# Local attention of a hybrid decoder: when the sixth query tile's weights are split, and how ten weight tiles get their low parts

## The chip, the cores and the metric

The kernel runs on one core of a Trainium2 chip. The metric is the device time of one execution in microseconds. Five engines work on queues of their own and meet only at semaphores: TensorE (PE, with its weight loads as PEld), VectorE (DVE), ScalarE (ACT), GpSimd (POOL) and SyncE (SP). SP issues nearly all transfers; POOL issues those that add what they carry onto what lies at their destination.

## The reference, cut to what matters

The model is a two-layer decoder over 528 tokens (16 of them meta tokens) of width 1024. Each layer is a feed-forward block, a token mixer and another feed-forward block. The mixer of the second layer is sliding-window attention over 128 tokens, with keys and values made earlier, and the change lies in its query and output projections:

```python
def swa_mixer(hn, w_q, sinks, w_out, k, v, cos, sin):
    q = (hn @ w_q).reshape(B, L, N_KV_HEADS, GROUP, HEAD_DIM)
    q = (apply_partial_rope(q, cos, sin) * (HEAD_DIM ** -0.5)).transpose(0, 2, 3, 1, 4)
...
    s = jnp.einsum('bkgnqd,bknsd->bkgnqs', q_blk, k_band)
...
    p = sink_softmax(s, mask, sink_b[None, :, :, None, None, None])
    o_real = jnp.einsum('bkgnqs,bknsd->bkgnqd', p.astype(v.dtype), v_band).reshape(B, N_KV_HEADS, GROUP, S, HEAD_DIM)
    o = jnp.concatenate([o_meta, o_real], axis=3).transpose(0, 3, 1, 2, 4).reshape(B, L, N_Q_HEADS * HEAD_DIM)
    return o @ w_out
```

Everything is float32. The kernel gets that precision from TensorE by splitting each operand into a high part, which TensorE takes in its fast float32 form (fp32r), and a low part, the rest: a product is then high by high, low by high and high by low, three matrix products.

## The kernel before, in words

**Weights.** All weights are cut into units in the order of their use (`units`). Here a unit is a tile of 128 by 1024 numbers: one query tile (`w_q`, eight of them, two heads each) or one tile of the output weights (`swa_out`, eight). A unit comes from memory by SP into two raw tiles of 512 columns (`load_unit`, L293; there are 11 raw tiles). Each half is then split by `split_part` (L235): ACT copies the raw half into the high part of a new tile (L237), DVE subtracts that from the raw half into the low part (L238). These tiles `w` come from a pool of 32 slots, which also holds queries, scores and other work.

**The planner.** The program is written out in full when the kernel is built. `Flow` (L64) is a clock that matrix products advance by an assumed cost (`mm`, L164: 512 columns of fp32r cost 512/2400 us), and a heap of jobs that fall due at times of that clock. What is due is written into the program between the products (`flow.pump`, after every three products of a unit). The engines' queues therefore hold the work in about the order of the due times; a scheduler may move an instruction that isn't ready behind later ones.

`split_unit` (L241) is the job of one unit: 2.2 us after the assumed end of its transfer it falls due, it may have to wait for the operand `x.built[1]`, for a gap of 2.2 us to the half before it (`gap[0]`, which is GAP from L1337 on), and for room (`slot`, L225). Room is a count of half-tiles: `set_ahead(n)` (L220) lets the planner ask for n halves beyond those that were given back by `done_w` (L347), and hold n at a time. `next_w` (L325) takes the next unit for TensorE; the planner's clock goes on, and other due jobs are written out, until that unit's job is done.

**The stage.** `swa` (L1213) calls `set_ahead(10)`, then `x_first` (L500) for the first four query tiles: their weights are there, `set_ahead(2 * first_ahead)` with first_ahead=5 leaves room for one tile more, the fifth, whose split waits for `x.built[1]`. The first four tiles are multiplied for two groups of 256 tokens, which follow each other as the normalized input is built; then `done_w(4)` gives eight halves of room, and `x_units` (L477) multiplies tiles five to eight for all 512 tokens, eight times three products of 512 columns each. Tiles that are done go through `rope` (L1150): DVE shuffles and multiplies by cosines (L1153, L1154), POOL multiplies by sines and adds (L1155, L1156). POOL's rope of the second token group needs the cosines and sines `csq`, which DVE has first to scale with the norm of that group (L1231).

`soft` (L1244) is one query tile's scores and softmax: four blocks of score products `sc` (one step of two products each), their reduction on DVE (L1267), exponentials on ACT (L1274), and the multiplication by the inverse sum (L1290), one head on DVE and the other on POOL. `core` (L1292) transposes the result on TensorE (`pt`, `pp`, L177), copies it (L1309, L1310) and multiplies by the values (`o`). The first scores fall due 2.0 us after the ropes of the first four tiles, so scores, query products and later transposes and output products stand mixed in TensorE's queue. `out_proj` (L551) multiplies by the output weights, in two halves of four units each.

**Transfers that add.** The feed-forward blocks already use them: `split_pair` (L254) builds sums of two weight blocks with `onto`, a transfer issued by POOL with `accum_op=ALU.add` (L270).

Of the kernel before, what the change touches and what calls it, by code (L numbers as in the profile page):

```python
# [9 lines left out]
F32 = mybir.dt.float32  # L10
F32R = mybir.dt.float32r
I32 = mybir.dt.int32
AF = mybir.ActivationFunctionType
ALU = mybir.AluOpType
# [4 lines left out]
KD = 8  # L19
# [108 lines left out]
def trunk_kernel(ctx: ExitStack, tc, a, out):  # L128
    nc = tc.nc
    pe, act, dve, pool, sp = nc.tensor, nc.scalar, nc.vector, nc.gpsimd, nc.sync  # L130
    flow = Flow()
# [15 lines left out]
    def ps(name):  # L147
        return pp.tile([P, 512], F32, tag="ps", name=name)

    def pair_tile(name, dt=F32R):  # L150
        return hp.tile([P, 2, TOK], dt, tag="pair", name=name)
# [8 lines left out]
    def gain(layer, i, k):  # L160
        c = V_GAIN + layer * 48 + i * 8 + k
        return vec[:, c : c + 1]
# [19 lines left out]
    gap, turn = [0.0], [0.0]  # L182
# [6 lines left out]
    units = []  # L189
    for layer in range(2):  # L190
        for f in range(2):
            for lo, hi in FF_CHUNKS:
                for t in range(lo, hi):
                    pair = [a["w_in"][layer, f, t, 0], a["w_in"][layer, f, t, 1]]
                    units += pair if lo == 0 else [pair]
                if lo < LAST:
                    units += [a["w_out"][layer, f, m, :, lo * P : hi * P] for m in range(KD)]
                else:
                    units += [a["w_last"][layer, f, i] for i in range(NLAST)]
            if f == 0 and layer == 0:  # L200
                units += [a["gla_in"][u] for u in GLA_ORDER]
                units += [a["gla_out"][m] for m in range(KD)]
            elif f == 0:
                units += [a["w_q"][u] for u in range(KD)]
                units += [a["swa_out"][i] for i in range(KD)]
            elif layer == 0:
                units += [a["w_kv"][u] for u in range(4)]

    costs = [7 if isinstance(u, list) else -(-u.shape[-1] // 512) for u in units]
    loaded = []  # L210
# [9 lines left out]
    def set_ahead(n, slots=None):  # L220
        ahead[0], limit[0] = n, slots or n
        room[0].finish(flow)
        room[0] = Job(None)

    def slot(i):  # L225

        while live[0] + sum(n for j, n in owed.items() if j < i) >= limit[0]:
            yield room[0]
        live[0] += 1
        owed[i] -= 1  # L230

    def raw_tile(name):
        return rp.tile([P, 512], F32, tag="raw", name=name)

    def split_part(i, raw, m):  # L235
        w = pair_tile(f"w{i}_{len(loaded[i])}")
        act.activation(w[:, 0, :m], raw[:, :m], AF.Copy)  # L237
        hold(dve.tensor_tensor(w[:, 1, :m], raw[:, :m], w[:, 0, :m].bitcast(F32), op=ALU.subtract))  # L238
        loaded[i].append(w)

    def split_unit(i, raws, x):  # L241
        yield 2.2
        if x is not None:
            yield x.built[1]
        for raw, m in raws:
            if gap[0]:
                turn[0] = max(turn[0] + gap[0], flow.clock)
                yield turn[0] - flow.clock
            yield from slot(i)
            bound[0] = x and x.low  # L250
            split_part(i, raw, m)
            bound[0] = None
# [66 lines left out]
    def prefetch():  # L319
        while len(loaded) < cap[0] and asked[0] + costs[len(loaded)] <= freed[0] + ahead[0]:  # L320
            if isinstance(units[len(loaded)], list) and chains[0] == CHAINS:
                break
            load_unit()

    def next_w():  # L325
        used[0] += 1
        prefetch()
        flow.until(lambda: len(loaded) >= used[0])
        flow.wait(split_jobs[used[0] - 1])
        return loaded[used[0] - 1]  # L330
# [16 lines left out]
    def done_w(n=1):  # L347
        free_slots(sum(costs[released[0] : released[0] + n]))
        released[0] += n
# [150 lines left out]
    def x_first(x, nu, evac, opening=False, behind=(), first_ahead=8):  # L500
        behind = list(behind)
        ws = [] if opening else [next_w() for _ in range(nu)]
        set_ahead(8 if opening else 2 * first_ahead)
        jobs = []

        def drain(gi, g, some, pst):
            yield x.rjob[gi]
            if not opening:
                yield x.built[1]
            for i, p in zip(some, pst):  # L510
                bound[0] = None if opening else x.low
                evac(i, g, p)
                bound[0] = None
                yield 0.6

        both = range(nu)
        order = [(0, both[: nu // 2]), (0, both[nu // 2 :])] if opening else [(0, both)]
        for gi, some in order + [(1, both)]:
            g = x.groups[gi]
            n = g[1]  # L520
            while len(ws) <= some[-1]:
                ws.append(next_w())
            shared = n <= 256
            if shared:
                banks = [ps(f"x{used[0]}_{i}_{gi}") for i in some[::2]]
                pst = [banks[i // 2][:, i % 2 * 256 : i % 2 * 256 + n] for i in range(len(some))]
            else:
                pst = [ps(f"x{used[0]}_{i}_{gi}")[:, :n] for i in some]
            for k in range(KD):
                if k == 1 and not opening and gi == 1:  # L530
                    cap[0] = len(units)
                    behind_x[0] = x
                    prefetch()
                x.need(gi, k)
                mm3s([(p, ws[i]) for i, p in zip(some, pst)], k, x.tiles[k], g, k == 0, k == KD - 1, shared)
            behind_x[0] = None
            flow.until(lambda: x.rjob[gi] is not None)
            jobs.append(flow.spawn(drain(gi, g, some, pst)))
            if opening and gi == 0 and some[-1] == nu - 1:
                cap[0] = len(units)  # L540
                prefetch()
            if behind:
                flow.spawn(behind.pop(0))
        done_w(nu)
        return jobs
# [666 lines left out]

    def swa(x, kv, finish):  # L1213
        kz, vt, vmz = kv
        set_ahead(10)
        with tc.tile_pool(name="ap", bufs=1) as ap:
            away = ap.tile([P, WIN], F32, name="away")
            sp.dma_start(away, a["away"])
# [112 lines left out]
                softs.append(flow.spawn(soft(u, [*after, *softs[max(u - 2, 0) : max(u - 1, 0)]])))  # L1331
                cores.append(flow.spawn(core(u)))

            drained = x_first(x, 4, evac, first_ahead=5)
            for u in range(4):
                attend(u, *drained)
            gap[0] = GAP  # L1337
# [15 lines left out]
    x = Operand("l0f0", lambda k: gain(0, 0, k), L0)  # L1353
# [19 lines left out]
    raws = [[raw_tile(f"raw{i}_{c}") for c in (0, 512)] for i in range(2)]  # L1373
# [33 lines left out]
    x = nxt  # L1407
    nxt, fin = into("l0f1", 0, 3, False, lambda k: gain(0, 4, k), L0)
    gla(x, fin)
    x = nxt  # L1410
# [4 lines left out]
    with tc.tile_pool(name="kp", bufs=1) as kp:  # L1415
        x = Operand("l1f0", lambda k: gain(1, 0, k), L1)
# [11 lines left out]
        x = nxt  # L1428
# [96 lines left out]
```

## Time and profile before

| | us |
|---|---|
| median of three runs (1869.71 to 1871.39) | 1869.87 |
| the profiled execution, its own time | 1868.85 |
| its span, first instruction to last | 1867.0 |
| TensorE busy in the span | 1848.1 |
| DVE busy in the span | 1349.2 |
| ACT busy in the span | 1002.0 |
| POOL busy in the span | 315.2 |

The profile is of one execution. Times in its views are microseconds from the start of the span. L165 is the line of the helper that makes every matrix product, so products are told apart by their tiles: `x<-x_l1m,w` are the query products of this stage (those of 512 columns belong to tiles five to eight), `sc` the scores, `pt` and `pp` the transposes, `y<-so,w` the output projection. In the same way `w<-raw` at L237 and L238 are the two instructions of a split. The stage's query products begin at 1350.69 and its last output products end near 1506.

### The profile page before, as it was taken

To read this page: it belongs to the slowest core of one execution; us is meant where nothing else is said; L and a number is where in the kernel's file an instruction comes from. 1 tells how busy PE (TensorE), PEld (TensorE's weight loads), DVE (VectorE), ACT (ScalarE), POOL (GpSimd) and SP (SyncE) were. 2 spreads that over 40 slices of the span, in tenths; PEclk is the share of its full clock that TensorE was granted. 3 is DMA by queue.
4 is the path that set the end of the run, shared out by engine and by line. 5 is a ranking of instruction groups with operands and counts; after the bars stand their busy time and mean duration, and the time that the engine had idled before them with its cause. 6 is when DMAs were issued, how large, how long until landed. Compare 5 with 4: busy or idle time off the path is not lost.

```text
span 1867.0 us, 36799 instructions
## 1 busy us (share of the span) xinstructions
PE 1848.1 (99%) x14158; PEld 1762.7 (94%) x14158; DVE 1349.2 (72%) x2679; ACT 1002.0 (54%) x2179; POOL 315.2 (17%) x370
## 2 busy tenths in 40 slices
PE   8999999999999999999999999999999999999998
PEld 8999999999999999999999898989977898989897
DVE  7884757786574988484789685758799589858484
ACT  6662636564465666262665563636556566626363
POOL 2101010320001310101033011010353231010101
PEclk9999999999999999999999999999999999999999
DMA  5655655312113255555652356565411215565561
GB/s 198 146 152 143 153 147 159 125 58 80 46 58 114 69 136 154 137 150 149 163 165 58 102 150 161 145 161 158 131 56 48 80 37 134 161 150 155 145 175 46
DMA packets 132528, 231.31 MB, mean 124 GB/s; under 512 B 14848, under 2 KB 26624, under 8 KB 132352
## 3 DMA queue, kind: packets, MB, share of 16 engines
q1 hardware_dynamic: 111328, 191.07, 32.2%
q0 software_dynamic: 20736, 37.76, 12.9%
q8 instruction: 111, 1.82, 0.4%
q14 instruction: 65, 0.53, 0.1%
q10 hardware_dynamic: 288, 0.13, 0.0%
HBM read 226.80 MB, written 2.10 MB: 123 GB/s over the span
## 4 chain that ended last, share of the span: by engine, by line
PE 89%; DVE 6%; ACT 3%; issue 1%; DMA 0%; POOL 0%; SPq 0%; DVEq 0%; ACTq 0%; POOLq 0%
PE y L165 29%; PE a L165 21%; PE x L165 17%; PE c L165 10%; PE d L165 5%; PE o L165 1%; PE e L165 1%; PE yt L165 1%; PE po L165 1%; DVE w L238 1%; ACT w L237 1%; PE sc L165 1%; DVE H L457 1%; PE ps L165 0%; PE pt L177 0%
## 5 line engine op out<-in xcount | busy, mean ns | idle before, releaser
L270 POOL DMA_DIRECT2D raw<-in_w_in x144 | 125.8, 940 | 973.8 <-DMA raw<-in_w_in 366.1
L165 PE MATMUL y<-hidl0f,w 128*128 128x256 f32 (+1 forms) x2112 | 260.4, 285 | 0.0
L165 PEld LDWEIGHTS y<-hidl0f,w 128*128 128x128 f32 x2112 | 258.6, 188 | 0.2
L238 DVE TENSOR_TENSOR w<-raw,w 128x512 fp32r<-128x512 f32 x376 | 241.3, 669 | 23.6 <-ACT w L237 21.4
L265 DVE TENSOR_TENSOR w_s<-raw,w_s 128x512 fp32r<-128x512 f32 x288 | 195.3, 689 | 80.5 <-ACT w_s L264 78.3
L264 ACT ACTIVATE w_s<-raw 128x512 fp32r<-128x512 f32 x288 | 177.6, 625 | 110.4 <-DVE raw L280 69.9
L165 PE MATMUL y<-hidl1f,w 128*128 128x512 f32 (+1 forms) x1200 | 233.1, 354 | 0.0
L165 PEld LDWEIGHTS y<-hidl1f,w 128*128 128x128 f32 x1200 | 195.1, 188 | 32.8 <-DVE w L238 0.3
L237 ACT ACTIVATE w<-raw 128x512 fp32r<-128x512 f32 x376 | 206.6, 586 | 33.6 <-PE y L165 27.9
L265 DVE TENSOR_TENSOR w<-raw,w 128x512 fp32r<-128x512 f32 x216 | 145.6, 688 | 37.1 <-ACT w L264 35.1
L264 ACT ACTIVATE w<-raw 128x512 fp32r<-128x512 f32 x216 | 130.5, 621 | 46.5 <-PE y L165 45.4
L165 PE MATMUL x<-x_l0m,w 128*128 128x272 f32 (+1 forms) x1152 | 151.9, 289 | 0.0
L165 PEld LDWEIGHTS x<-x_l0m,w 128*128 128x128 f32 x1152 | 143.4, 188 | 1.6 <-ACT R_l0m L375 0.4
L585 DVE TENSOR_TENSOR Y<-y,Y 128x256 f32<-128x256 f32 (+2 forms) x160 | 75.6, 479 | 83.8 <-PE y L165 83.6
L165 PE MATMUL a<-zl0f_t,w_s 128*128 128x264 f32 x864 | 117.2, 285 | 0.0
L165 PE MATMUL a<-zl1f_t,w_s 128*128 128x256 f32 x864 | 114.6, 282 | 0.6 <-ACT c L878 0.4
L165 PEld LDWEIGHTS a<-zl0f_t,w_s 128*128 128x128 f32 x864 | 110.1, 188 | 0.0
L165 PEld LDWEIGHTS a<-zl1f_t,w_s 128*128 128x128 f32 x864 | 107.2, 188 | 1.7 <-ACT c L878 1.6
L394 POOL TENSOR_TENSOR acc_post<-acc_post,sq_post 128x256 f32<-128x256 f32 (+1 forms) x72 | 61.2, 850 | 275.8 <-ACT sq_post L393 272.9
L165 PE MATMUL x<-x_l0f,w 128*128 128x256 f32 (+1 forms) x768 | 98.3, 290 | 6.8 <-ACT w L237 5.9
L165 PEld LDWEIGHTS x<-x_l0f,w 128*128 128x128 f32 x768 | 96.4, 192 | 7.7 <-ACT w L237 5.9
L165 PE MATMUL x<-x_l1f,w 128*128 128x256 f32 (+1 forms) x576 | 92.1, 320 | 0.0
(386 smaller groups left out, 3364.5 us busy)
## 6 DMA issues: line engine op xcount, KB each, us to landing
raw<-in_w_in SPq DMA_DIRECT2D x424, 256.0 KB, 3.7
raw<-in_w_in POOLq DMA_DIRECT2D x144, 256.0 KB, 4.8
raw<-in_w_out SPq DMA_DIRECT2D x96, 256.0 KB, 3.5
raw<-in_w_last SPq DMA_DIRECT2D x48, 256.0 KB, 3.4
raw<-in_gla_in SPq DMA_DIRECT2D x48, 256.0 KB, 3.1
raw<-in_w_out SPq DMA_DIRECT2D x64, 128.0 KB, 2.9
raw<-in_gla_out SPq DMA_DIRECT2D x16, 256.0 KB, 2.8
raw<-in_w_q SPq DMA_DIRECT2D x16, 256.0 KB, 3.9
```

The lines of the kernel that those rows point to most:

```text
L165: inst = pe.matmul(o, lhs, rhs, start=start, stop=stop, skip_group_check=onto)
L237: act.activation(w[:, 0, :m], raw[:, :m], AF.Copy)
L238: hold(dve.tensor_tensor(w[:, 1, :m], raw[:, :m], w[:, 0, :m].bitcast(F32), op=ALU.subtract))
L264: act.activation(w[:, 0, :512], src, AF.Copy)
L265: dve.tensor_tensor(w[:, 1, :512], src, w[:, 0, :512].bitcast(F32), op=ALU.subtract)
L270: pool.dma_start(dst, src, accum_op=ALU.add)
L394: pool.tensor_tensor(sums[0][:, :n], sums[0][:, :n], t[:, :n], op=ALU.add)
L457: dve.tensor_tensor(h, t, h, op=ALU.add)
L585: dve.tensor_tensor(y, p[:, :n], y, op=ALU.add)
```

## The change

The room in the attention stage grows from ten halves to twelve: `set_ahead(12)`, and first_ahead=6, so that the sixth query tile is asked for together with the fifth. Ten units (`lifted`: the last two query tiles, and the eight tiles of output weights) are no longer split by `split_part`. The new `lift` writes for each half the high part by ACT, as before, then by a second ACT copy of scale -1 the negated high part where the low part will lie, and has POOL issue a transfer that adds the weights from memory onto it: minus high plus weight is the low part. The halves of lifted units follow each other at 1.5 us of the planner's clock in place of the gap of 2.2 us, and a lifted unit counts as done 5.0 us after its last issue. The raw halves are still fetched by SP, since the high part is copied from them.

```diff
@@ -202,6 +202,7 @@
             elif f == 0:
                 units += [a["w_q"][u] for u in range(KD)]
+                lifted = range(len(units) - KD + 6, len(units) + KD)
                 units += [a["swa_out"][i] for i in range(KD)]
@@ -238,10 +239,25 @@
+    def lift(i, raws):
+        for c, (raw, m) in enumerate(raws):
+            turn[0] = max(turn[0] + 1.5, flow.clock)
+            yield turn[0] - flow.clock
+            yield from slot(i)
+            w = pair_tile(f"w{i}_{c}")
+            act.activation(w[:, 0, :m], raw[:, :m], AF.Copy)
+            act.activation(w[:, 1, :m], w[:, 0, :m].bitcast(F32), AF.Copy, scale=-1.0)
+            pool.dma_start(w[:, 1, :m], units[i][:, c * 512 : c * 512 + m].bitcast(F32R), accum_op=ALU.add)
+            loaded[i].append(w)
+        yield 5.0
+
     def split_unit(i, raws, x):
         yield 2.2
         if x is not None:
             yield x.built[1]
+        if i in lifted:
+            yield from lift(i, raws)
+            return
         for raw, m in raws:
@@ -1212,7 +1228,7 @@
         kz, vt, vmz = kv
-        set_ahead(10)
+        set_ahead(12)
         with tc.tile_pool(name="ap", bufs=1) as ap:
@@ -1331,7 +1347,7 @@
-            drained = x_first(x, 4, evac, first_ahead=5)
+            drained = x_first(x, 4, evac, first_ahead=6)
             for u in range(4):
                 attend(u, *drained)
```

## The prediction

> **What bounds the kernel now.** I read the page first: busy times, then the chain of work that ended last.
>
> ```profile
> span 1867.0 us, 36799 instructions
> PE 1848.1 (99%) x14158; PEld 1762.7 (94%) x14158; DVE 1349.2 (72%) x2679; ACT 1002.0 (54%) x2179; POOL 315.2 (17%) x370
> PE 89%; DVE 6%; ACT 3%; issue 1%; DMA 0%; POOL 0%; SPq 0%; DVEq 0%; ACTq 0%; POOLq 0%
> ```
>
> TensorE is busy 99% of the span and makes 89% of the chain. A change that takes no product away can win only where TensorE stands still, so the second view is what TensorE waited for: first in the whole span, then (the single line) between 1300 and 1430 us, around the sliding-window stage.
>
> ```profile
> PE x L165 <- ACT w L237: 5.9, 1, 5.9
> PE x L165 <- DVE w L238: 2.6, 4, 1.5
> PE sc L165 <- DVE q L1154: 0.7, 1, 0.7
> PE pt L177 <- DVE pt L1310: 0.2, 1, 0.2
> ```
>
> ```profile
> PE x L165 <- DVE w L238: 1.7, 2, 1.5
> ```
>
> The 5.9 us are the kernel's opening. In the stage of the change TensorE waits 1.7 + 0.7 + 0.2 = 2.6 us. The timeline of TensorE gives their places (start, duration, then in brackets the idle time before and who ended it):
>
> ```profile
> 1375.20 1.44 PE L165 MATMUL x<-x_l1m,w 128*128 128x512 f32 x5 [0.26 <-DVE w L238]
> ...
> 1384.18 0.97 PE L165 MATMUL sc<-kz,q 64*128 64x144 f32 x6
> 1386.62 2.13 PE L165 MATMUL x<-x_l1m,w 128*128 128x512 f32 x8 [1.48 <-DVE w L238]
> ...
> 1391.59 0.95 PE L165 MATMUL x<-x_l1m,w 128*128 128x512 f32 x3
> ...
> 1393.73 1.67 PE L165 MATMUL x<-x_l1m,w 128*128 128x512 f32 x6
> 1395.33 0.73 PE L165 MATMUL sc<-kz,q 64*128 64x272 f32 x4
> ...
> 1405.98 0.51 PE L165 MATMUL sc<-kz,q 64*128 64x144 f32 x2 [0.69 <-DVE q L1154]
> ...
> 1407.23 0.60 PE L177 MATMUL pt<-ident,Y 128*128 128x128 f32 x4
> ...
> 1413.17 0.55 PE L177 MATMUL pt<-ident,Y 128*128 128x128 f32 x3 [0.18 <-DVE pt L1310]
> ```
>
> Counting products from 1375 (24 to a query tile), the 1.48 us stand in the sixth tile, before its 13th product: TensorE waits for the low part of the second half of that tile's weights. The tenth-by-tenth windows (each engine's busy us, and the DMA share after the clock) say why it is late, and who has room:
>
> ```profile
> 1370.00:1380.00 10.00, 9.74 (x63) 8.56 (x62) 9.38 (x24) 5.17 (x11) 7.41 (x9) 1.00 0.19 52
> 1380.00:1390.00 10.00, 8.52 (x38) 5.87 (x36) 9.93 (x27) 1.99 (x6) 8.39 (x10) 1.00 0.25 77
> 1390.00:1400.00 10.00, 10.00 (x51) 6.15 (x49) 9.83 (x39) 9.24 (x32) 4.97 (x5) 1.00 0.36 118
> 1400.00:1410.00 10.00, 9.25 (x47) 5.61 (x47) 10.00 (x32) 6.12 (x21) 4.92 (x4) 1.00 0.24 72
> ```
>
> The columns are PE, PEld, DVE, ACT, POOL. DVE is full throughout; ACT has room, least in 1390:1400; POOL is nearly full where the ropes run; the DMA engines are two thirds idle. The clock is 1.00, so nothing here is throttling.
>
> **The change, part by part.** First DVE and POOL in that stretch, and ACT's long pause:
>
> ```profile
> 1377.57 0.40 DVE L1154 TENSOR_TENSOR q<-x,csq 128x256 f32<-128x256 f32 x1
> 1377.90 1.04 DVE L238 TENSOR_TENSOR w<-raw,w 128x512 fp32r<-128x512 f32 x1
> ...
> 1385.63 2.08 DVE L238 TENSOR_TENSOR w<-raw,w 128x512 fp32r<-128x512 f32 x2
> ```
>
> ```profile
> 1378.47 1.07 POOL L1156 TENSOR_TENSOR q<-q,sh_q 128x256 f32<-128x256 f32 x1
> ...
> 1380.32 0.74 POOL L1156 TENSOR_TENSOR q<-q,sh_q 128x256 f32<-128x256 f32 x1
> 1382.28 0.74 POOL L1155 TENSOR_TENSOR sh_q<-sh_q,csq 128x256 f32<-128x256 f32 x1 [1.22 <-DVE csq L1231]
> ...
> 1401.79 2.37 POOL L1290 TENSOR_TENSOR Y<-Y,den 128x144 f32<-128x144 f32 x2 [6.66 <-DVE mt L1287]
> 1405.43 1.27 POOL L1155 TENSOR_TENSOR sh_q<-sh_q,csq 128x512 f32<-128x512 f32 x1 [1.28 <-DVE sh_q L1153]
> 1406.78 1.29 POOL L1156 TENSOR_TENSOR q<-q,sh_q 128x512 f32<-128x512 f32 x1
> ```
>
> ```profile
> 1388.03 0.42 ACT L1274 ACTIVATE Y<-Y,nm 128x144 f32<-128x144 f32 x1 [7.08 <-DVE nm L1267]
> ```
>
> *Sixth tile sooner.* With room for twelve half-tiles instead of ten, both subtractions of the sixth tile follow the fifth's (at about 1376), ahead of the ropes of tiles 2 to 4. Before, they ran at 1377.90 and 1385.63; now both are done by about 1378.5, six us before use. The 1.48 us go.
>
> *Subtractions removed.* Two query tiles and eight output tiles of two halves each are 20 subtractions. At the mean of the whole run below that is 20 x 0.669 = 13.4 us off DVE.
>
> ```profile
> L238 DVE TENSOR_TENSOR w<-raw,w 128x512 fp32r<-128x512 f32 x376 | 241.3, 669 | 23.6 <-ACT w L237 21.4
> L237 ACT ACTIVATE w<-raw 128x512 fp32r<-128x512 f32 x376 | 206.6, 586 | 33.6 <-PE y L165 27.9
> ```
>
> ```profile
> L270 POOL DMA_DIRECT2D raw<-in_w_in x144: 853/865/1195, 55.8 to 1794.9; - x144
> DMA to landing us min/median/max: 3.7/4.8/8.0
> ```
>
> TensorE's two other waits on DVE, 0.69 and 0.18 us, lie behind some eight of these subtractions and should go as well. The 0.26 us belong to the fifth tile and stay.
>
> *Copies added on ACT.* 20 x 0.586 = 11.7 us. The first eight or so fall into ACT's 7.08 us pause; the others take the place that the first copies had among the exponentials. Cost 0; without that cover about 3 x 0.59 = 1.8 us of exponentials come later, in front of work that DVE now reaches sooner.
>
> *Transfers added.* 20 issues on POOL at 0.865 us (rows above; the Strassen weights use the same accumulating form) are 17.3 us of POOL, and each lands 4.8 us after its issue (3.7 to 8.0). Their bytes, 20 x 256 KB, are a second reading of the tiles in a stretch where the DMA engines are busy 0.19 to 0.36: 0. What counts is POOL's queue, which I follow. Two subtractions more before the ropes of the first token group delay those by 0.8 to 1.6 us (2 x 0.669 or 2 x 1.04, less the 0.5 us by which DVE led POOL: 1377.97 against 1378.47); I take 1.2, so they end at 1381.06 + 1.2 = 1382.3. By the due times in the code the seventh tile's first issue comes next, in the place where POOL waited 1.22 us for the cosines: 1383.2, landing 1387.1. The ropes of the second group (0.74 + 0.74 and a small gap, 1.55 a tile) follow; the first tile's is done at 1384.8, before TensorE, which now has 18 instead of 12 products of the sixth tile ahead of its first score (the planner held that tile 0.9 us for its second half, and does so no more), asks at 1384.18 + 6 x 0.24 = 1385.6. Cost 0; without those products 0.6. Tiles 2 and 3: 1387.9. Then the fifth tile's rope over all 512 tokens, 1.27 + 1.29 at the quiet row: 1390.4. Only behind it stands the issue for the seventh tile's second half; it lands at 1395.2.
>
> When is it needed? The seventh tile began at 1391.59. Without the 1.48 us it would be 1390.1; and the planner, which held it until its weights were due and put three score steps (0.65 us each, as from 1395.33 to 1395.99) there, now calls it due and goes on: 1388.1. The first half is there. Twelve products (1.60 for six with a score behind, from 1393.73 to 1395.33, so 3.2) and four score steps, one of them short (2.4): 1393.7. The second half is 1.5 us late (0.4 at a landing of 3.7, 4.7 at 8.0; nothing if the issue gets ahead of the fifth rope). I take 1.5, since the median is from 144 cases with fuller queues.
>
> *Who is behind these issues on POOL.* The fourth tile's rope, not urgent; then, after four issues, the sixth's rope, six more issues, and the softmax products of the first tile (L1290). 1391.3 + 1.55 + 3.5 + 2.6 + 5.2 = 1404.1, plus the two products at 1.0: 1406.1, against 1404.2 before. TensorE transposes them at 1407.23 - 1.48 - 0.69 + 1.5 = 1406.6. Cost 0, with 0.5 us to spare; if the 1.5 us were not lost, this wait would take 1.0 of them.
>
> *Order.* More score steps now stand between products. A run of six with a score behind takes 1.60 us; in the two rows below 21 in a run take 4.99, 1.43 for six. So a break costs 0.17; two more cost 0.3.
>
> ```profile
> 1465.96 5.15 PE L165 MATMUL y<-so,w 128*128 128x512 f32 x21
> 1470.95 0.60 PE L177 MATMUL pt<-ident,s 128*128 128x128 f32 x4
> ```
>
> Output weights have over 20 us between issue and use, and all that is after the stage runs as before: 0.
>
> **Sum:** -1.48 - 0.69 - 0.18 + 1.5 + 0.3 = -0.55 us. The profiled execution took 1868.85 us (span 1867.0 and 1.85 around it); that gives 1868.3. The median of the runs shown, 1869.87, lies 1.02 higher, so the forecast is 1869.3 us: no change that can be told, since a measurement of this kernel tells about 0.2%, 3.7 us.
>
> The fit of the Trainium skill (DMA: Bandwidth & Descriptors, Anatomy of one DMA) for transfers issued by GpSimd, 2.0 us plus bytes over 436e3, gives an estimate of 2.6 us for 256 KB, against 3.7 to 8.0 in the rows here, which add onto their destination; by it the half would land at 1393.0, in time, and the sum would be that of the first rival.
>
> **The rivals.** *No new wait.* The issue is placed ahead of the fifth rope, the half lands by 1392.7 and POOL keeps up: -2.35 us, 1867.5. For it: the engines' order within the program need not be the order of the due times. A better interleaving of the same products might give one to two us more (at 0.17 a break, ten breaks fewer), so this case ends at about 1865.8. Against: POOL's 7.41 and 8.39 of 10.
>
> *POOL becomes the bound (slower).* Place: the seventh tile's second half. If its issue stands behind the fourth rope too (1.55) and lands in 8.0, it is there at 1399.9, 6.2 us late: -2.35 + 0.3 + 6.2 = +4.2, 1874.1; each further pair of issues ahead of it adds 1.7, to about 1876. It decides from 2 us of lateness on; beyond 5.8 it is slower by over 0.2%. For it: POOL's two full windows. Against: ACT is early.
>
> *Issues stretched by DVE.* The 853/865/1195 row has a slow end. At 1.195 the twelve issues before the first tile's softmax products end 4.0 us later, 1410.1; TensorE waits 3.5 instead of 0: +3.0, 1872.8. For it: DVE full here; against: the median, 0.865, comes from stages in which DVE is busy as well. The Trainium skill (SBUF — State Buffer, SBUF: two separate sides) has the mechanism: while VectorE runs an operation that takes the port pair it shares with GpSimd, descriptors can't be written.
>
> *It doesn't do what it says.* The sixth tile's halves stay among the ropes, or the first score waits in their place for its rope: -0.87 + 0.3 + 1.0 and the rest as forecast, about 1870.5. Against: room is there when the fifth tile starts.
>
> **How the numbers follow.** Forecast 0.34 (own range 1867.8 to 1871.8); no new wait 0.26, of which 0.12 below 1866.1; POOL the bound 0.23, of which 0.19 above 1873.6; stretched issues 0.10, of which 0.06 above; swapped wait 0.07. Faster by over 0.2% 0.12, slower 0.25, within 0.63. The range is 1866.3 to 1875.2, leaving out about one tenth at each end.
>
> **What would show it.** No wait of products on DVE before 1400 except 0.26; a wait at the seventh tile on a transfer; POOL without its 6.66 us pause; DVE's windows from 1390 below 9; the transposes at 1406 to 1408. I am wrong if TensorE waits over 5 us for the seventh or eighth tile or the first tile's softmax, or if the stage's order changes by more than two or three breaks.

## The result, and the profile after

| | before | after |
|---|---|---|
| median, us (22 runs each) | 1869.59 (1869.03 to 1872.06) | 1872.72 (1871.05 to 1873.34) |
| the profiled execution, us | 1868.85 | 1872.67 |
| its span, us | 1867.0 | 1870.8 |
| TensorE's granted clock, mean over the span | 0.999 | 0.997 |

The ratio is 1.0014, 95% interval 1.0008 to 1.002: 1.5 to 3.7 us slower, where 0.55 us faster was the sum. The measured median lies inside the stated range of 1866.3 to 1875.2, but the change went the other way. The medians differ by 3.1 us, the spans of the two profiled executions by 3.8 us.

From the page of the changed kernel, and from its table of groups by line, the load on the engines:

```profile
span 1870.8 us, 36828 instructions
PE 1849.3 (99%) x14158; PEld 1763.7 (94%) x14158; DVE 1337.5 (71%) x2659; ACT 1012.0 (54%) x2199; POOL 331.0 (18%) x390
L239 DVE TENSOR_TENSOR w<-raw,w 128x512 fp32r<-128x512 f32 x356 | 225.7, 663 | 23.0 <-ACT w L238 20.7
```

Twenty subtractions are gone (376 to 356, 241.3 - 225.7 = 15.6 us; DVE as a whole is busy 11.7 us less), with twenty issues more on POOL and ten us more on ACT. What TensorE waits for, whole span (us in total, times, longest):

```profile
PE x L165 <- DMA w<-in_w_q: 3.5, 1, 3.5
...
PE x L165 <- DVE w L239: 1.1, 3, 0.6
PE pt L177 <- DVE nm L1283: 1.0, 1, 1.0
PE o L165 <- ACT pt L1325: 0.6, 1, 0.6
```

The longest of the waits on VectorE for weights was 1.5 and is 0.6: the sixth tile's wait is gone. A wait of 3.5 us on an adding transfer has come. TensorE's timeline (start, duration, then the idle time before and who ended it), query products and four groups of scores:

```profile
1375.22 1.43 PE L165 MATMUL x<-x_l1m,w 128*128 128x512 f32 x5 [0.27 <-DVE w L239]
1376.73 8.68 PE L165 MATMUL x<-x_l1m,w 128*128 128x512 f32 x36
...
1388.02 1.65 PE L165 MATMUL x<-x_l1m,w 128*128 128x512 f32 x6
1389.60 0.97 PE L165 MATMUL sc<-kz,q 64*128 64x272 f32 x8
...
1392.51 1.20 PE L165 MATMUL x<-x_l1m,w 128*128 128x512 f32 x4
1397.19 1.22 PE L165 MATMUL x<-x_l1m,w 128*128 128x512 f32 x2 [3.48 <-DMA w<-in_w_q]
1398.34 1.28 PE L165 MATMUL sc<-kz,q 64*128 64x272 f32 x4
1399.55 2.93 PE L165 MATMUL x<-x_l1m,w 128*128 128x512 f32 x6
1402.41 1.61 PE L165 MATMUL sc<-kz,q 64*128 64x272 f32 x8
1403.94 1.66 PE L165 MATMUL x<-x_l1m,w 128*128 128x512 f32 x6
1405.53 0.73 PE L165 MATMUL sc<-kz,q 64*128 64x272 f32 x4
```

The fifth tile and the first half of the sixth, and on into its second half, are 36 products in one run. The seventh tile's second half is asked for at 1392.51 + 1.20 = 1393.7 and there at 1397.19. The rows behind the wait are the surprise: six products take 2.93 us and then 1.66, four score products 1.28 us and then 0.73. The windows say why (PE, PEld, DVE, ACT, POOL in busy us, then the granted clock, the DMA share and GB/s):

```profile
1390.00:1400.00 10.00, 6.52 (x30) 3.62 (x27) 4.00 (x19) 9.22 (x29) 9.92 (x13) 0.85 0.89 188
1400.00:1410.00 10.00, 10.00 (x46) 6.59 (x47) 7.15 (x33) 6.37 (x21) 6.31 (x8) 0.81 1.12 236
...
1394.00:1396.00 2.00, 0.00 (x0) 0.00 (x0) 0.01 (x1) 2.00 (x9) 2.00 (x3) 1.00 1.01 216
1396.00:1398.00 2.00, 0.81 (x2) 0.50 (x2) 0.00 (x0) 2.00 (x8) 1.92 (x2) 0.73 1.11 183
1398.00:1400.00 2.00, 2.00 (x6) 0.96 (x6) 0.35 (x1) 1.22 (x4) 2.00 (x5) 0.50 1.09 253
1400.00:1402.00 2.00, 2.00 (x6) 1.37 (x5) 0.86 (x6) 1.80 (x6) 2.00 (x3) 0.50 1.12 277
1402.00:1404.00 2.00, 2.00 (x11) 1.22 (x9) 0.28 (x1) 0.35 (x1) 0.48 (x1) 0.57 1.09 262
1404.00:1406.00 2.00, 2.00 (x12) 1.29 (x10) 2.00 (x10) 1.64 (x5) 0.00 (x0) 1.00 1.14 212
```

TensorE's granted clock falls to half near the end of the wait and stays there while TensorE is busy. How long: a window of 2 us at 0.73 has (1 - 0.73) x 2 / 0.5 = 1.08 us of half clock, one at 0.57 has 1.72, so 1.08 + 2 + 2 + 1.72 = 6.8 us, to about 1403.7. TensorE was back from 1397.19, so 6.5 us of work ran at half speed: 3.3 us lost. DVE, meanwhile, is idle (4.00 of 10, from 9.83).

POOL's timeline shows where the deciding transfer stood:

```profile
1382.08 0.88 POOL L250 DMA_DIRECT2D w<-in_w_q  x1
...
1387.89 1.30 POOL L1171 TENSOR_TENSOR sh_q<-sh_q,csq 128x512 f32<-128x512 f32 x1
1389.27 1.29 POOL L1172 TENSOR_TENSOR q<-q,sh_q 128x512 f32<-128x512 f32 x1
1390.51 0.74 POOL L1171 TENSOR_TENSOR sh_q<-sh_q,csq 128x256 f32<-128x256 f32 x1
1391.20 0.87 POOL L250 DMA_DIRECT2D w<-in_w_q  x1
...
1398.03 4.45 POOL L250 DMA_DIRECT2D w<-in_swa_out  x5
1406.17 1.93 POOL L1306 TENSOR_TENSOR Y<-Y,den 128x144 f32<-128x144 f32 x2 [3.69 <-DVE mt L1303]
```

Issued at 1391.20, behind the fifth tile's rope, and usable at 1397.19: 6.0 us.

**The account of the 3.8 us.** Waits of the stage before: 0.26 + 1.48 + 0.69 + 0.18 = 2.61; after: 0.27 + 3.48 + 1.03 + 0.59 = 5.37 (the last two are the waits for `nm` and `pt` above). That is 2.8 us more; the half clock is 3.3 us; together 6.1. So 2.3 us came back elsewhere, and most of it can be seen in the score products. They took this much of TensorE in the stage before (the one row of a window on that tile):

```profile
1375.00:1445.00 70.00, 19.87 (x112) 10.08 (x112) 22.42 (x54) 1.00 0.23 69
```

and after, the same 112 products, in spite of the half clock:

```profile
1375.00:1449.00 74.00, 18.84 (x112) 10.11 (x112) 22.47 (x55) 0.95 0.58 129
```

That is 1.0 us less. Two of the groups after stand in the half clock: 1.28 us where four score products take 0.73 at the full clock, and 1.61 us where eight take 0.97, together 1.2 us of loss. At the full clock the score products would thus have taken about 2.2 us less than before, an estimate from these rows. Without the half clock, the change as a whole would have come out at 3.8 - 3.3 = +0.5 us.

### The profile page after: what moved, and what is told of

Its sections match the earlier page's. It is cut to its first block, busy times and chain, and to the rows that moved or that the text cites. A ratio compares the mean times of both kernels' runs of the same rounds, so it can differ in the third digit from the quotient of the medians.

```text
span 1870.8 us, 36828 instructions
## 1 busy us (share of the span) xinstructions
PE 1849.3 (99%) x14158; PEld 1763.7 (94%) x14158; DVE 1337.5 (71%) x2659; ACT 1012.0 (54%) x2199; POOL 331.0 (18%) x390
## 4 chain that ended last, share of the span: by engine, by line
PE 88%; DVE 6%; ACT 3%; issue 1%; DMA 1%; POOL 1%; SPq 0%; DVEq 0%; ACTq 0%; POOLq 0%
PE y L165 29%; PE a L165 21%; PE x L165 17%; PE c L165 9%; PE d L165 5%; PE e L165 1%; PE yt L165 1%; PE o L165 1%; PE po L165 1%; ACT w L238 1%; DVE H L473 1%; PE sc L165 0%; PE ps L165 0%; DVE w L239 0%; DMA w<-in_w_q 0%
## 5 line engine op out<-in xcount | busy, mean ns | idle before, releaser
L239 DVE TENSOR_TENSOR w<-raw,w 128x512 fp32r<-128x512 f32 x356 | 225.7, 663 | 23.0 <-ACT w L238 20.7
L238 ACT ACTIVATE w<-raw 128x512 fp32r<-128x512 f32 x356 | 194.6, 584 | 33.6 <-PE y L165 27.9
L281 DVE TENSOR_TENSOR w<-raw,w 128x512 fp32r<-128x512 f32 x216 | 145.6, 688 | 37.2 <-ACT w L280 34.2
L280 ACT ACTIVATE w<-raw 128x512 fp32r<-128x512 f32 x216 | 130.6, 621 | 46.6 <-PE y L165 44.0
```

Source lines behind the costliest of these rows:

```text
L280: act.activation(w[:, 0, :512], src, AF.Copy)
L281: dve.tensor_tensor(w[:, 1, :512], src, w[:, 0, :512].bitcast(F32), op=ALU.subtract)
```

## The experiments

Times are medians, beside runs of the kernel before on the same chip; in brackets the 95% interval of the ratio. "Half clock" is a stretch at 0.50, its length worked out from windows as above or read from the granted clock on record in the trace.

**1. Which part of the change costs?** Four kernels, each a part of the change. The first has only the new room and the earlier sixth tile, with nothing lifted:

```diff
-                lifted = range(len(units) - KD + 6, len(units) + KD)
+                lifted = range(0)
```

> The kernel before with the greater room alone (twelve halves, the sixth tile asked for with the fifth); no half gets its low part by a transfer. Theory (the loss is one late transfer, the second half of the seventh query tile, 3.48 us of waiting, and half of TensorE's clock for some 6 us after it): neither is here, the 1.48 us wait of the sixth tile is gone, the other waits on DVE (0.69, 0.18) stay or move; clock 1.00 from 1390 to 1410; 1 to 2 us faster than before. Rival A (the greater room itself costs, because ropes and scores come later behind two more subtractions): as slow as before or 1 to 3 us slower, with new waits of scores between 1384 and 1400.

The second lifts only the output weights, `lifted = range(len(units), len(units) + KD)`, the third only the two query tiles, `lifted = range(len(units) - KD + 6, len(units))`, both with the new room:

> The change with the adding transfers for the eight tiles of output weights alone; the last two query tiles are split by DVE as before. Theory: no wait on a transfer in the query tiles, clock 1.00 throughout, four fewer issues on POOL early on; 1 to 2.5 us faster than before. Rival B (POOL's queue as a whole is too long, and the first tile's softmax products and the transposes behind it pay): transposes wait 1 us or more, time from before to 2 us slower. Rival C (the DMA engines are overfull between 1394 and 1410 by the output tiles): DMA share stays near 1 there and the time within 1 us of before.

> The change with the adding transfers for the last two query tiles alone; the output weights are split by DVE as before. Theory: the second half of the seventh tile is still issued behind the rope of the fifth tile, about 1391, and lands 4 to 5 us later without the output tiles' transfers beside it: a wait of 1.5 to 3 us; if it is under about 3 us the clock stays at 1.00 and the time is within 1.5 us of before, if it is over 3.4 the clock halves and the time is 2 to 4 us above. Rival C (the lateness is the crowd of output transfers): the wait is under 1 us and the time 1 us or more below before.

The fourth lifts all ten units, with the old room (`set_ahead(10)`, first_ahead=5):

> All ten units by adding transfers, with the room of before (ten halves, the sixth tile not asked for with the fifth). Theory: the sixth tile's wait of about 1.5 us is back, the seventh tile's halves are issued later still against the ropes, since the sixth tile's are first to be given room; the wait for its second half is 2 to 6 us, with the clock halved where it is over 3.4; 2 to 6 us slower than before. Rival A (the room is what costs): within 1 us of before or faster.

| | median (before: 1869.32) | ratio | longest waits of the stage, us | half clock, us |
|---|---|---|---|---|
| room only | 1874.74 | 1.0026 [1.0016, 1.0036] | 2.00 + 1.49; 1.03 | 6.8; 3.4 |
| output weights only | 1871.89 | 1.0009 [1.0000, 1.0018] | 3.58 | 6.8 |
| query tiles only | 1876.56 | 1.0033 [1.0021, 1.0046] | 3.18; 1.50; 1.11 | 6.8; 3.4; 3.4 |
| lift only | 1873.54 | 1.0018 [1.0009, 1.0026] | 1.52; 3.12 | 6.8 |

The waits, from TensorE's timelines: room only,

```profile
1407.23 1.35 PE L165 MATMUL sc<-kz,q 64*128 64x272 f32 x6 [2.00 <-DVE q L1170]
1410.07 0.84 PE L165 MATMUL sc<-kz,q 64*128 64x144 f32 x2 [1.49 <-DVE nm L1283]
```

output weights only,

```profile
1408.33 0.84 PE L165 MATMUL sc<-kz,q 64*128 64x144 f32 x2 [3.58 <-DVE nm L1283]
```

and query tiles only:

```profile
1397.54 1.22 PE L165 MATMUL x<-x_l1m,w 128*128 128x512 f32 x2 [3.18 <-DMA w<-in_w_q]
```

No part alone is faster than before. The expectations for the first three missed: room only and output weights only were to be faster, and query tiles only was to be at most 4 us slower, where it was 7.2. Lift only was within its 2 to 6 us. Two things follow. First, query tiles only leaves out the sixteen transfers of the output weights, and the wait is still 3.18 us. There the second half was issued at 1392.15 and usable at 1397.54, 5.4 us against 6.0 after the change: the crowd of output transfers is worth about 0.6 us, by one execution of each, and the place in POOL's queue and the transfer's own length the rest. Second, with nothing late by transfer (room only, output weights only) other waits of 2 to 3.6 us come, on VectorE's queries and maxima (`q` and `nm` in the views), while VectorE is busy 9.93 of the 10 us from 1400 to 1410 in both. A likely reading is that products and scores reach TensorE in another order once the planner no longer holds the sixth tile, and that VectorE, which still has subtractions of other tiles to do, is late with what the scores need; no run tests that by itself. Each of the four has a wait of over 1.9 us, and a half clock at it.

**2. The second half sooner.** The seventh tile's two issues follow each other without the 1.5 us on the planner's clock, so that both stand ahead of the ropes; then the same with the old room:

```diff
-            turn[0] = max(turn[0] + 1.5, flow.clock)
+            turn[0] = max(turn[0] + (0.0 if i == lifted[0] else 1.5), flow.clock)
```

> The changed kernel, but the two halves of the seventh query tile are written out together, without 1.5 us between them, so that both issues stand on POOL ahead of the ropes of the second token group. Theory (the loss is that late second half, 3.48 us of waiting plus half of TensorE's clock for 6 us, some 3.2 us): the second issue is at about 1383, lands by 1390, no wait on a transfer in the seventh tile, clock 1.00 between 1390 and 1404; the first score waits up to 0.9 us for its rope; 3 to 6 us faster than the changed kernel, 0 to 3 us faster than before. Rival (a wait taken away here comes back elsewhere, since DVE or POOL bound the stage; in the run with the greater room alone DVE's waits came back as 5.5 us): a new wait of over 2 us at the eighth tile, a score or a transpose, and a time within 1.5 us of the changed kernel.

> As the run before in this list, but with the room of the kernel before (ten halves, the sixth tile not asked for with the fifth). Theory: the sixth tile's wait of 1.5 us is back, the seventh tile's second half lands in time or under 1 us late, clock 1.00; 1 to 3 us slower than with the greater room, within 1.5 us of before. Rival (the greater room turns the planner's order against TensorE): faster than with the greater room.

With the new room: 1872.42 beside 1869.40 (1.0012 [1.0003, 1.0021]). Both issues went out together at 1382.53 and the wait for the transfer is gone. From TensorE's timeline, what is left of waits:

```profile
1406.44 0.55 PE L177 MATMUL pt<-ident,Y 128*128 128x128 f32 x3 [0.68 <-POOL Y L1306]
1410.57 1.01 PE L165 MATMUL sc<-kz,q 64*128 64x272 f32 x4 [1.33 <-DVE nm L1283]
1412.61 0.73 PE L177 MATMUL pt<-ident,Y 128*128 128x128 f32 x3 [1.03 <-DVE nm L1283]
```

and the window that follows:

```profile
1410.00:1420.00 10.00, 8.40 (x56) 6.85 (x56) 7.23 (x28) 4.20 (x17) 5.59 (x6) 0.66 0.71 149
```

The first row is the wait that the prediction set down for the case in which no time is lost at the seventh tile (POOL late with the first tile's softmax; 1.0 there, 0.68 here). The others are VectorE's softmax. None is over 1.4 us, and still (1 - 0.66) x 10 / 0.5 = 6.8 us of half clock follow. Not in every execution: two of the eleven runs have a recorded mean clock of 0.999 and took 1869.50 and 1869.52, the other nine have 0.997 or 0.998 and took 1872.06 to 1873.45. About 3 us lie between executions of one and the same kernel, which fits the 3.3 us that a half clock of 6.8 us costs. With the old room it was 1875.97 (1.0032 [1.0019, 1.0044]): both issues then stood together *behind* the ropes, at 1391.55, and TensorE waited for 6.79 us, with 10.2 us of half clock (1392.45 to 1402.69). Both expectations missed: the first kernel was to be 3 to 6 us faster than the changed one, and in the second the half was to be under 1 us late. Moving the issue alone doesn't settle the matter.

**3. What does a wait of a known length cost?** To the kernel before, nothing else changed, a chain of additions on POOL (a number nobody uses) and a 16-column matmul that waits for it, in the output projection, where TensorE doesn't wait otherwise. With one, two or five additions:

```diff
+                if finish.name == "l1f1" and gi == 0 and m == 3:
+                    late = sm.tile([P, 256], F32, tag="late", name="late", bufs=1)
+                    y = Y[:, m, g[0] : g[0] + 256]
+                    pool.tensor_tensor(late, y, y, op=ALU.add)
+                    for _ in range(1):
+                        pool.tensor_tensor(late, late, late, op=ALU.add)
+                    pe.matmul(ps("late")[:, :16], ones, late[:, :16], start=True, stop=True)
```

(the range is 0, 1 or 4)

> The kernel before, with one addition on GpSimd and a 16-column matmul that waits for it, in the output projection, where before TensorE never waits. With two additions the wait was 1.96 us and a half clock of 3.4 us followed; with five it was 4.59 us, and a half clock of 6.8 us; (4.59 - 1.96) / 3 = 0.88 us an addition, so here the wait is about 1.1 us. If any wait of 1 us in a window halves the clock: 1.1 + 0.25 + 1.7 = +3.0 us, 1872.4, half clock of 3.4 us behind it. If the share of the window must be larger (over about a half): no half clock, +1.3 us, 1870.7.

> The kernel before with one short wait of TensorE put in among the output products after the attention (near 1490 us), where no other engine is full: a matrix product of 16 columns waits for a chain of two additions on POOL that starts from the products just before it. Expected wait about 2.2 us. If a wait costs its own length alone: 2 to 2.6 us slower than before, clock 1.00. If a wait of this length already halves the clock: 4.5 us or more slower, with a granted clock of 0.5 to 0.8 in the windows behind it. The theory expects the first.

> The same with a chain of five additions on POOL, a wait of about 4.5 us. Theory (a wait of 3.5 us halves TensorE's clock for the 6 us after it): 7 to 8.5 us slower than before, the granted clock near 0.5 for 6 to 7 us after the wait. Rival (the half clock of the changed kernel comes from elsewhere, such as the crowd of transfers or the kind of products behind the wait): 4.3 to 5 us slower and clock 1.00.

| additions | wait, us | half clock, us | median beside before | us more [interval] |
|---|---|---|---|---|
| 1 | 1.27 | none | 1870.99, 1869.51 | 1.5 [-0.4, 2.8] |
| 2 | 1.96 | 3.4 | 1873.27, 1869.40 | 3.9 [1.9, 5.4] |
| 5 | 4.59 | 6.8 | 1876.17, 1869.40 | 6.8 [4.5, 9.5] |

The windows of the kernel with two additions (the first row is the stage of the change; then the place of the added wait):

```profile
1385.00:1395.00 10.00, 8.18 (x31) 4.70 (x30) 8.35 (x20) 4.22 (x12) 8.89 (x9) 0.83 0.26 79
1490.00:1492.00 2.00, 0.59 (x5) 0.39 (x4) 1.05 (x2) 0.78 (x2) 1.52 (x4) 1.00 0.98 363
1492.00:1494.00 2.00, 1.45 (x9) 1.45 (x9) 0.00 (x0) 0.00 (x0) 1.18 (x2) 0.76 0.83 294
1494.00:1496.00 2.00, 2.00 (x11) 2.00 (x11) 0.42 (x1) 0.00 (x0) 0.00 (x0) 0.50 0.01 4
1496.00:1498.00 2.00, 2.00 (x17) 2.00 (x17) 0.42 (x1) 0.46 (x2) 0.74 (x1) 0.88 0.00 0
```

0.96 + 2 + 0.48 = 3.4 us of half clock, begun when TensorE had started again. The added matmul holds the next product up by 0.24 us (it begins at 1492.55 and the next product at 1492.79). The wait, this and half of 3.4 us make 1.96 + 0.24 + 1.7 = 3.9 us, as measured. With five additions TensorE came back at 1495.9 and the clock at 1500.4, 4.5 us of work at half speed: 4.59 + 0.24 + 2.2 = 7.0 us against 6.8. With one, the wait alone: 1.27 + 0.25 = 1.5, as measured, though that interval reaches below zero. So the shortest wait cost its length, and the longer two cost 1.7 and 2.2 us more. That 1.96 us would be enough was not expected. Nor, it seems, was it enough in every execution: one of the ten runs with two additions has a recorded mean clock of 0.999, and at 1871.66 it lies 2.3 us above before, about the wait and its matmul alone.

The first row is a find of its own. There, at the unchanged 1.5 us wait of the sixth tile, this execution has (1 - 0.83) x 10 / 0.5 = 3.4 us of half clock. The profile of before, with the same instructions and the same wait, has none. The 22 times of the kernel before fall in two groups, fourteen from 1869.0 to 1869.9 and eight from 1870.4 to 1872.1. The mean granted clock that is on record for each run tells what the groups are: of the 79 runs of the kernel before that stand beside the experiments, 55 have 0.999 or 1.000 and took 1868.62 to 1870.29 (median 1869.23), and 24 have 0.997 or 0.998 and took 1870.69 to 1872.03 (median 1871.24); no run lies between 1870.29 and 1870.69. A half clock of 3.4 us lowers the mean by 0.5 x 3.4 / 1867 = 0.0009 and costs 1.7 us, against 2.0 between the medians. So the kernel before, too, has such a half clock in about three executions of ten. At which wait it comes there, no profile of such a run shows.

**4. Fewer lifted, old room.** With the old room, the output weights alone; and the output weights with the eighth query tile, `lifted = range(len(units) - KD + 7, len(units) + KD)`:

> Only the eight output tiles get their low parts by adding transfers; room stays ten, the first tile's five, as before the change. So the sixth tile's second half stays among the ropes (a wait of about 1.5 us on VectorE) and no query tile hangs on a transfer. Theory A (the change loses by the late transfer of the seventh tile and by the halved clock behind that wait): neither arises here, VectorE has up to 16 subtractions less after 1400, the waits of 0.69 and 0.18 us may go: 1868.7 to 1869.6, ratio 0.9995 to 1.0000, no stretch of half clock. Theory B (the stage is bound by VectorE's softmax, and a new order of scores and products makes TensorE wait whatever is lifted): a wait of scores or transposes on VectorE of over 1.5 us comes, with a half clock of 3.4 or 6.8 us behind it: 1871 to 1873.

> The eighth query tile and the eight output tiles are lifted, the seventh and all before it by subtraction; room ten and five as before. Theory A: the eighth tile is first asked for about 6 us after the seventh's, and its first issue on POOL no longer stands behind another tile's; it lands in time or under 1 us late, no half clock: 1868.3 to 1869.6, ratio 0.9993 to 1.0000. Theory C (any query tile by adding transfers is late, since its second issue falls behind a rope on POOL): a wait of 2 to 4 us at the eighth tile on the transfer, a half clock of 6.8 us behind it: 1873 to 1875.

1873.54 (1.0018 [1.0009, 1.0027]) and 1872.26 (1.0010 [1.0001, 1.0019]), beside 1869.51. No transfer is late in either, and neither is faster. In the first TensorE waits at the sixth tile as before (1.54) and then 1.37 for a query on VectorE, with 3.4 us of half clock in the profiled execution; that one took 1870.68 with a mean clock of 0.999, and nine of the other ten have 0.996 to 0.998 and took 1871.88 to 1874.98, so they had more half clock than this profile shows. Neither expectation for it fits: the first had no half clock, the second a wait of over 1.5 us on a score. In the second:

```profile
1386.59 2.12 PE L165 MATMUL x<-x_l1m,w 128*128 128x512 f32 x8 [1.54 <-DVE w L239]
...
1408.81 0.73 PE L165 MATMUL sc<-kz,q 64*128 64x272 f32 x4 [1.90 <-ACT pt L1325]
```

a wait for a copy on ACT, which has the high parts and the negated ones to make among the exponentials, and 6.8 us of half clock. That ACT's added copies, put at 0 in the prediction, cost something here is likely, but no run takes them away. Again the half clock doesn't come in every execution: three of the eleven runs have a mean clock of 0.999 and took 1870.05 to 1870.22, the other eight 0.997 and 1871.11 to 1872.80. Neither expectation for this kernel foresaw a wait on ACT.

**5. The wait filled with other work.** The changed kernel, with one number other than in it: the planner counts the seventh tile as there 9 us after its second issue, not 5. Then it writes score steps ahead of that tile.

```diff
-        yield 5.0
+        yield 9.0 if i == lifted[0] else 5.0
```

> The changed kernel, but the planner counts the seventh tile's weights as there 9 us after the second issue instead of 5, so that score steps stand ahead of its second half. Theory A: the wait of 3.48 us is filled with score steps that TensorE has to do anyway, no half clock follows: 3.5 + 3.2 us less than the changed kernel, 1865.7 to 1867, ratio 0.998 to 0.999. Theory B: the scores come earlier than VectorE can take their maxima, TensorE waits there instead (2 to 4 us in waits of scores on VectorE between 1390 and 1410) and the clock halves for 3.4 or 6.8 us: 1871.5 to 1874.

1866.35 (1866.07 to 1867.02) beside 1869.51: ratio 0.9982 [0.9973, 0.999], and the span is 1864.4. It is faster than before by 3.2 us, and the changed kernel was 3.1 us slower than before. POOL's issue of the second half, and TensorE's timeline:

```profile
1391.30 0.87 POOL L250 DMA_DIRECT2D w<-in_w_q  x1
```

```profile
1387.51 2.89 PE L165 MATMUL sc<-kz,q 64*128 64x272 f32 x20
1391.00 1.63 PE L165 MATMUL x<-x_l1m,w 128*128 128x512 f32 x6 [0.60 <-DVE q L1170]
...
1395.72 0.49 PE L165 MATMUL x<-x_l1m,w 128*128 128x512 f32 x1
1396.86 1.42 PE L165 MATMUL x<-x_l1m,w 128*128 128x512 f32 x5 [0.64 <-DMA w<-in_w_q]
```

The issue is at 1391.30 (1391.20 in the changed kernel) and the half is there at 1396.86 (1397.19). The transfer is as late as it was; TensorE merely asks for it at 1396.2 and not at 1393.7, since twenty score products, in one run, now stand ahead of the tile. The windows of the stage:

```profile
1390.00:1400.00 10.00, 8.76 (x41) 5.39 (x40) 9.26 (x37) 10.00 (x31) 9.92 (x13) 1.00 0.85 165
1400.00:1410.00 10.00, 10.00 (x54) 5.89 (x54) 9.78 (x42) 10.00 (x39) 9.92 (x11) 1.00 1.11 249
```

The clock stays at 1.00, with DMA as crowded and POOL fuller than in the changed kernel, and DVE back at work (9.26 for 4.00). The stage's waits are 0.25 + 0.60 + 0.64 = 1.5 us, 1.1 less than before. The score products took

```profile
1375.00:1445.00 70.00, 18.19 (x112) 9.79 (x112) 23.20 (x56) 1.00 0.60 136
```

1.7 us less than before. 1.1 + 1.7 = 2.8, against 2.6 between the spans. The medians are 3.2 us apart, partly because nine of the 33 runs of before beside it have a mean clock of 0.997 or 0.998; the median of the other 24 is 1869.25, 2.9 us above. All eleven runs here have 0.999 or 1.000 and lie within 1 us.

## Why the prediction was wrong, point by point

- **Sixth tile sooner: right.** The run of 36 products has no wait, and the first wait of products on VectorE is the fifth tile's 0.27.
- **Subtractions removed: right** (15.6 us off their group and 11.7 off DVE as a whole, for 13.4), but with another end. The two waits of 0.69 and 0.18 are gone from their places, and waits of 1.03 and 0.59 on `nm` and `pt` came later in the stage: where the sum had -0.87, it was 1.62 - 0.87 = +0.75.
- **POOL's queue: right but for 0.8 us.** The first issue of the seventh tile began at 1382.08 for 1382.3 (1383.2 was its end), usable in time; the fifth tile's rope ended at 1390.56 for 1390.4; then a 0.74 us step of another rope got ahead, and the second issue came at 1391.20 for 1390.4. The first tile's softmax on POOL was done at 1408.1 for 1406.1, with no wait of TensorE for it; POOL had stood idle for 3.69 us before it, waiting for DVE, so its own queue was not what came late.
- **"The second half is 1.5 us late": the term that was mis-sized.** TensorE asked at 1393.7, as worked out to the tenth, in part by luck: it began the seventh tile at 1388.02 for 1388.1 and then made thirteen products, not twelve (the first of the second half needs only the high part), while the four score steps were shorter than reckoned. The half came at 1397.19 for 1395.2: 0.8 from the issue and 1.2 from the transfer, which took 6.0 us and not the 4.8 of the median. 3.48 us, well within the bounds of 0 to 4.7. The reason given for not going above the median ("fuller queues" elsewhere) was wrong: the DMA engines were at 0.89 and 1.12 here, where before had 0.36 and 0.24. The change itself filled them, and SP's raw loads came earlier too. Of that crowd, only the output weights' transfers were taken away by a run (0.6 us off the transfer).
- **"The clock is 1.00, so nothing here is throttling": the step that failed.** It was read off the kernel before, for a kernel with another wait. In the sum, lateness was priced at its length. The 3.48 us wait brought 6.8 us of half clock, 3.3 us lost, nearly as much again. With the wait measured but the price of lateness kept, the prediction's sum would have been -0.55 + 1.98 = +1.4 us, plus 1.03 and 0.59 = +3.1; the clock is what made it +3.8, in spite of the 2.3 us that came back elsewhere, where the sum had lost 0.3. With all else as it was, a full clock would have left about +0.5 us. The sign that the prediction set for being wrong, a wait of over 5 us, didn't come; 3.48 us was enough. The added waits showed that price by itself, and the run with the due time of 9 us took wait and half clock away together and moved the kernel by 6 us.
- **Order: the wrong sign.** +0.3 for breaks; the score products came out 1.0 us shorter even with the half clock, 1.7 without. The 112 score products stand in 20 groups, against 21 before, where two breaks more were forecast; one group less, at 0.17, doesn't explain the gain. Why scores are cheaper in this order was not followed further.
- **The rivals.** The slower one, POOL as the bound, had the right place and mechanism, and the wrong price: it let 2 us of lateness be the point from which the change is slower, as a wait costs its length. The last experiment reached the time of *No new wait*, 1866.35 between its 1867.5 and its 1865.8, but by another way: the half landed as late as after the change, and TensorE asked later. *Issues stretched by DVE* isn't what cost: single issues do last up to 2.25 us in the profile, but they overlap (five in 4.45 us, 0.89 each), DVE was busy 4.00 of 10 us there, and POOL stood idle before the softmax products that this rival makes late. *It doesn't do what it says* is ruled out by the run of 36 products. The Trainium skill's gate rule (TensorE: Matmul & The Clock Gate, HAM oscillation) speaks of gaps above 3.4 us. The 3.48 us wait agrees with it, but 1.96 us was enough in the run with two additions.

## What to carry to other kernels

A wait of TensorE isn't priced by its length alone: from between 1 and 2 us on a half clock may come with it, here worth 1.7 to 3.3 us, and from 2 us on it did in every profile here. Look at the granted clock of each window behind every wait that a change may bring. If a transfer must be late, let TensorE ask later: one due time, with work put in front that had to be done anyway, turned 3.1 us of loss into 3.2 us of gain, while lifting fewer tiles or issuing the transfer sooner only moved the wait. Take a transfer's landing time from queues as full as the change will make them, not from the median of emptier ones.

## What the runs showed of the hardware that was not expected

- The half clock comes in lengths of 3.4 us and multiples: 3.4 (two added additions and the sixth tile's wait, among others), 6.8 (after the change and in seven experiments), 10.2 (the 6.79 us wait). Within one execution starts and ends lie on one grid: with the query tiles alone, by the granted clock on record in the trace, the stretches begin or end at 1396.81, 1403.64, 1413.88, 1417.29, 1434.36 and 1437.77, which are 0, 2, 5, 6, 11 and 12 steps of 3.41 us. The Trainium skill (TensorE: Matmul & The Clock Gate, Part 1: The HAM clock gate) has such a free-running window of 3413 ns, and this agrees with it.
- What it takes in a window isn't a full window of idleness. 1.96 us did it in one run, and so did 1.33 and 1.03 together; a lone 1.27 and, in the changed kernel, a lone 1.03 did not; the sixth tile's 1.5 did in two executions and did not in six others, and a 1.03 late in the room-only kernel was followed by 3.4 us.
- Where the wait falls on the grid makes part of that difference. Every execution ends with a half clock, since TensorE has nothing to do in the last 6.5 us, and its start gives the grid of that execution, steps of 3.413 us back from there. In the two executions in which the sixth tile's 1.50 us brought a half clock, the wait lay whole in one step, and the half clock began with the next. In five of the six others it was divided between two steps, with at most 1.35 us in one; in the sixth (lift only) 1.52 us lay in one step and the clock stayed. Over all fourteen traces, from 20 us on and before the kernel's last 10 us, every step at full clock with 1.6 us or more of idle TensorE was followed by half clock and none with less than 1.0 was; from 1.03 to 1.52 both happened.
- The half clock lasts a second step mostly when TensorE is idle in the first. In all seven stretches of one step TensorE had no idle time in that step. In six of the eight of two steps the wait reached into the first, by 0.28 to 2.37 us (0.28 in the changed kernel). In the other two (both halves together, and the eighth tile with the old room) TensorE was busy throughout and the clock still stayed at half for a second step; what decides there stays open.
- An adding transfer of 256 KB issued by POOL took 6.0 us to be usable with the DMA engines at 0.9 to 1.1, and the one issued at 1391.30 in the last experiment took 5.6. All twenty of the changed kernel took 4.0 to 11.1 us to land, median 5.7, where the prediction took 4.8 from a row of 3.7 to 8.0.
